# Other PSUM banks for the projections of the gated linear attention, and an earlier place in the program for five decode and mask loads

## The chip, the core and the metric

The kernel runs on one core of a Trainium2 chip. Its engines take their instructions each in a fixed order: PE (TensorE, matrix products into PSUM), DVE (VectorE), ACT (ScalarE), POOL (GpSimd) and SP (SyncE, which issues most DMAs). They wait for one another through semaphores. PSUM has 8 banks of 128 x 512 fp32, and a tile of it can be written only once the tile that lay in its bank has been read. The metric is the device time of one execution in microseconds (us).

## The reference, cut to what matters

One step of a hybrid decoder layer over a prompt of 2048 tokens and 8 samples of 8 new tokens with 4096 past tokens each. Model width 1024.

```
z = rmsnorm(h) @ w_in            # q_c, kv_c, gate_mla | q_g, k_g, v_g, a_g, gate_gla
# MLA: 8 heads, scores over 64 + 32 dims, values of 64
q_nope, q_rope = split(rmsnorm(q_c) @ w_qup);  c_kv = rmsnorm(kv_c);  k_rope = rope(kv_c)
prompt:  k = c_kv @ w_uk;  v = c_kv @ w_uv;  o = softmax(causal(q k + q_rope k_rope)) v
decode:  q_lat = q_nope @ w_uk;  c = cache_ckv[page_table], kr = cache_krope[page_table]
         o_lat = softmax(mask(q_lat c + q_rope kr)) c;  o = o_lat @ w_uv
# GLA: 4 heads, dk 64, dv 128, chunks of 64 tokens, S the carried state
o = (q exp(b)) S + A v;  S = exp(b_last) S + (k exp(b_last - b))^T v;  o = rmsnorm(o) * silu(gate)
h += concat(o_mla * silu(gate_mla), o_gla) @ w_out
h += sigmoid(h @ w_ple_gate) * (p @ w_ple_proj);  y = rmsnorm(h)
```

Outputs are y for both groups, the new latent and rotary rows, and the new GLA states.

## The kernel before, in words

The program has five stages, one after the other:

- pass_a, 0 to some 355 us: input projection for the MLA part, latents, q, k and v, which are written to DRAM (Qn, Qr, Kn, Kr, Vd).
- pass_b, to some 753 us: the GLA. For 17 tiles (16 of 128 prompt tokens, one of 64 sample tokens) inproj computes three projections of 512 columns (PSUM tiles pgB, lines 64 to 66), and gla does the chunked recurrence with PSUM tiles ptB and poB. The last step of a tile is mg (line 691, on DVE), the gated and normalised output, which SP stores to DRAM (MGd, line 692). Its factor comes from ACT (686) and POOL (91, 92). The final states go out by line 648.
- attention, first part, and decode, to some 1080 us. attention loads keys KT (lines 898 and 905), values VT (906) and queries qC (911, 912). For every head and block of 512 queries it first finds the row maxima of the scores (maxima: product on PE, line 925, into pmC; reduction on DVE, 927 to 932; the maxima are turned by PE, 940, and copied by ACT into row 96 of qC, 941), and then computes scores (955 to 957, psC), exponentials (959, 961) and outputs (968 to 970, poC). decode works on 16 chunks of 2048 past tokens: ct (latent pages, each by a DMA from SP whose address is read from the page table ptab, 764 and 769), cr and kt (indirect gathers of POOL, 771 and 775, with indices computed from pt_i and p16 at 731 to 735), products 783 and 787 into ptD. Ahead of that it needs qlat, a product of the sample queries with ukT (742), and qrs, 32 copies on DVE (750). The driver gives 3.2 attention steps for each decode step.
- attention alone, to some 1345 us.
- output, to the end: output projection, the gated embedding, the last norm.

PSUM pools take banks in the order in which they are opened, those of attention from the other end. So in pass_b pgB has banks 0 to 2, ptB 3 to 6 and poB 7; behind it ptD has 0 and 1, poD 2, poC 3, psC 4 and 5, and pmC 6 and 7.

The written order of the code is not the order on the engines. A scheduler takes all instructions of the program, with their data and buffer dependences and its own estimate of when each could run, and writes one list for every engine; a DMA into memory that no one has used can be placed anywhere ahead of its reader. On SP a DMA also waits until the one eight places ahead in its lane has landed.

Of the kernel before, what the change touches and what calls it, by code (L numbers as in the profile page):

```python
# [14 lines left out]
F32 = mybir.dt.float32  # L15
F32R = mybir.dt.float32r
I32 = mybir.dt.int32
# [4 lines left out]
PSUM = bass.MemoryType.PSUM  # L22
DRAM = bass.MemoryType.DRAM

P = 128
# [4 lines left out]
NB, TD = 8, 8  # L30
SD = NB * TD
T = S + SD
PAST = 4096
H, DN, DR, DV = 8, 64, 32, 64
CL, QL = 128, 256
# [11 lines left out]
def emit(ctx, tc, I, O):  # L47
    nc = tc.nc
# [54 lines left out]
    keep = ctx.enter_context(tc.tile_pool(name="keep", bufs=1))  # L103
# [339 lines left out]

    def pass_b(ws, xp, wb):
        with ExitStack() as c:
            wp = pool(c, "cB", 1)
            sp = pool(c, "sB", 2)
            s1 = pool(c, "s1B", 1)
            pg = pool(c, "pgB", 3, PSUM)
            pt = pool(c, "ptB", 4, PSUM)  # L450
            po = pool(c, "poB", 1, PSUM)

            def xsplit(i, m):
# [242 lines left out]
            for cnt, (i, m) in enumerate(order):  # L696
                x, x1 = x1, None
                gla(cnt, i, m, *cur)
                if cnt + 1 < len(order):
                    if cnt + 2 < len(order):  # L700
                        x1 = xsplit(*order[cnt + 2])
                    cur = inproj(x, *order[cnt + 1])
                if cnt + 2 == len(order):
                    wb.close()


    def decode(c):

# [8 lines left out]
        HP = 8  # L717
        ukT = wp.tile([P, 4, CL], F32, name="ukT")
        nc.sync.dma_start(ukT, I["w_ukT"])
        uv = wp.tile([P, H, DV], F32, name="uv")  # L720
        nc.sync.dma_start(uv, I["w_uv"].rearrange("c (h d) -> c h d", h=H))
        nmask = wp.tile([SD, NB, SD], F32, name="nmask")
        nc.sync.dma_start(nmask, I["nmask"])
        ptab = wp.tile([1, NB * 32], I32, name="ptab")
        nc.sync.dma_start(ptab, I["page_row"])
        pt_i = wp.tile([P, NB * 6 * NCK], I32, name="pt_i")
        nc.sync.dma_start(pt_i, I["pages"])
        p16 = wp.tile([P, 2], I32, name="p16")
        nc.sync.dma_start(p16, I["p16"])
        idx = wp.tile([P, NB * 2 * NCK], I32, name="idx")  # L730
# [131 lines left out]
        for n, (b, ck) in enumerate(chunks):  # L862
            cur = ld.pop(0)
            if n + 2 < len(chunks):
                ld.append(load(*chunks[n + 2]))
            if ck == 0:
                st = (sp.tile([SD, N], F32, name="mxD"), sp.tile([SD, N], F32, name="dnD"), sp.tile([SD, N, CL], F32, name="oc"))
            yield from chunk(b, ck, *cur, *st)
            if ck == NCK - 1:
                yield from fresh(b, *st)  # L870
                yield from combine(b, *st)
# [9 lines left out]

    def attention(c, we, slots):

# [6 lines left out]
        po = pool(c, "poC", 1, PSUM, side="right")  # L890
        cm = wp.tile([P, P], F32, name="cm")
        nc.sync.dma_start(cm, I["cmask"])

# [136 lines left out]
    def output(c, slots, close):  # L1030
# [118 lines left out]
            for n, (i, m) in enumerate(tiles):  # L1149
# [4 lines left out]
                hN = nx  # L1154

    with ExitStack() as wb:
        ws, xp = pass_a(wb)
        pass_b(ws, xp, wb)
    with ExitStack() as e:
        c = ExitStack()  # L1160
        slots = []
        att = attention(c, e, slots)
        next(att)
        with ExitStack() as d:
            dec = decode(d)
            acc = 0.0
            for _ in dec:
                acc += DEC_RATE
                while acc >= 1:
                    next(att, None)  # L1170
                    acc -= 1
        for _ in att:
            pass
        output(e, slots, c.close)
# [102 lines left out]
```

## Time and profile before

| | us |
|---|---|
| median of 3 runs | 1880.7 (1877.29 to 1881.57) |
| profiled execution | 1881.52 |
| its span, first to last instruction | 1879.5 |
| PE busy | 1749.4 (93%) |
| DVE busy | 1080.3 (57%) |
| ACT busy | 781.7 (42%) |
| POOL busy | 532.3 (28%) |
| mean granted clock of PE | 0.955 |

The span is 2.0 us shorter than the execution's time, and every time of the trace counts from its start. In a timeline a row has its start, its duration, the engine, the line of the kernel, the operation, the tile written and the tiles read (without the number of the buffer) and, in brackets, how long the engine stood idle ahead of it and what ended that. "issue" there means that the profile shows nothing that was waited for, "remote" a signal that it could not trace.

### The profile page before, as it was taken

Reading aid. Unit: us, or ns where it says so; the run is one execution under the profiler, and the core shown is the slowest. Engines: PE = TensorE matmul, PEld = TensorE weight load, DVE = VectorE, ACT = ScalarE, POOL = GpSimd, SP = SyncE. Lnnn points to the kernel's source line nnn. Section 1 sums busy time; section 2 is a strip of 40 time slices with the busy share of each in tenths; the row PEclk is TensorE's granted clock in tenths of the full one; section 3 lists DMA queues with packets and bytes.
Section 4 is the critical chain, followed back from the end, with each engine's and each line's share of the span. In section 5 each row is a group of like instructions: output and inputs, shape, how many; then the busy total and the mean of one; then the engine's idle time right before and its main releaser. Section 6 shows DMA issues by size and latency. Waiting matters only on the chain.

```text
span 1879.5 us, 26843 instructions
## 1 busy us (share of the span) xinstructions
PE 1749.4 (93%) x8928; PEld 1365.5 (73%) x8928; DVE 1080.3 (57%) x2359; ACT 781.7 (42%) x1896; POOL 532.3 (28%) x915
## 2 busy tenths in 40 slices
PE   4999987899999998499999999999999999999996
PEld 3877776688887786266666777777777888888884
DVE  6376476466653666466666687777777333333323
ACT  4354365343431433055554666766661212121212
POOL 5253253333442334424343011111136000000000
PEclk7999989899999998699999999999998999999998
DMA  5164475511111114655666243123334223322111
GB/s 170 40 241 140 163 272 183 170 42 40 45 40 48 32 35 121 195 157 155 184 172 171 62 129 89 49 69 77 91 84 147 89 75 88 95 85 82 56 49 34
DMA packets 187748, 200.53 MB, mean 107 GB/s; under 512 B 23290, under 2 KB 130668, under 8 KB 187612
## 3 DMA queue, kind: packets, MB, share of 16 engines
q1 hardware_dynamic: 180956, 177.86, 32.3%
q0 software_dynamic: 6656, 20.98, 3.6%
q8 instruction: 71, 1.16, 0.3%
q14 instruction: 65, 0.53, 0.1%
HBM read 142.42 MB, written 56.35 MB: 106 GB/s over the span
## 4 chain that ended last, share of the span: by engine, by line
PE 70%; DMA 3%; DVE 3%; issue 2%; SPq 1%; POOL 1%; ACT 1%; POOLq 0%; ACTq 0%; DVEq 0%
PE pgE L64 7%; PE pgE L66 7%; PE pgE L65 7%; PE pgB L66 4%; PE pgB L64 4%; PE pgB L65 4%; PE psC L955 3%; PE poC L968 3%; PE pmC L925 3%; PE poC L970 3%; PE psC L957 3%; PE psC L956 3%; PE poC L969 3%; PE ptD L783 2%; PE poD L82 1%
## 5 line engine op out<-in xcount | busy, mean ns | idle before, releaser
L959 ACT ACTIVATE ph<-psC 128x512 fp32r<-128x512 f32 (+1 forms) x320 | 171.5, 536 | 206.1 <-PE psC L957 90.1
L963 DVE TENSOR_TENSOR pl<-pf,ph 128x512 fp32r<-128x512 f32 (+1 forms) x320 | 191.3, 608 | 58.5 <-ACT pf L961 49.2
L961 ACT ACTIVATE pf<-psC 128x512 f32<-128x512 f32 (+1 forms) x320 | 170.9, 534 | 0.0
L927 DVE TENSOR_REDUCE mxC<-pmC 128x1 f32<-128x512 f32 x192 | 128.9, 684 | 54.0 <-PE pmC L925 38.1
L955 PE MATMUL psC<-qC,KT 97*128 97x512 f32 (+1 forms) x320 | 124.1, 388 | 15.4 <-issue 11.8
L966 POOL TENSOR_SCALAR_AFFINE_SELECT ph<-ph 128x128 fp32r<-128x128 f32 x128 | 43.3, 339 | 322.5 <-DVE pl L963 228.0
L968 PE MATMUL poC<-ph,VT 128*128 128x512 f32 (+1 forms) x320 | 124.3, 388 | 8.8 <-POOL ph L966 6.7
L925 PE MATMUL pmC<-KT,qC 96*128 96x512 f32 (+2 forms) x320 | 119.2, 399 | 10.1 <-issue 4.6
L970 PE MATMUL poC<-pl,VT 128*128 128x512 f32 (+1 forms) x320 | 122.0, 382 | 1.3 <-DVE pl L963 1.3
L956 PE MATMUL psC<-qC,KT 96*128 96x512 f32 (+1 forms) x320 | 119.6, 374 | 0.0
L957 PE MATMUL psC<-qC,KT 96*128 96x512 f32 (+1 forms) x320 | 119.5, 373 | 0.0
L969 PE MATMUL poC<-ph,VT 128*64 128x512 f32 (+1 forms) x320 | 118.1, 369 | 0.0
L955 PEld LDWEIGHTS psC<-qC,KT 97*128 97x128 f32 x320 | 61.3, 192 | 38.4 <-issue 13.4
L1139 DVE SCALAR_TENSOR_TENSOR thE<-thE,pgE 128x512 f32<-128x512 f32 x32 | 22.0, 688 | 114.3 <-ACT thE L1138 114.3
L64 PE MATMUL pgE<-wpg,hh 128*128 128x512 f32 x224 | 87.7, 392 | 0.0
L65 PE MATMUL pgE<-wpg,hh 128*128 128x512 f32 x224 | 87.7, 392 | 0.0
L925 PEld LDWEIGHTS pmC<-KT,qC 96*128 96x128 f32 x320 | 62.6, 198 | 32.3 <-issue 11.0
L1138 ACT ACTIVATE thE<-pgE 128x512 f32<-128x512 f32 x32 | 19.1, 598 | 160.6 <-PE pgE L66 160.6
L66 PE MATMUL pgE<-wpg,hl 128*128 128x512 f32 x224 | 85.3, 392 | 0.0
L968 PEld LDWEIGHTS poC<-ph,VT 128*128 128x128 f32 x320 | 62.7, 196 | 29.0 <-POOL ph L966 13.4
L775 POOL DMA_INDIRECT kt<-in_kropeT,idk x64 | 61.5, 961 | 65.5 <-PE ptD L787 49.5
L61 DVE TENSOR_TENSOR x<-x 128x512 fp32r<-128x512 f32 (+2 forms) x74 | 64.6, 917 | 22.8 <-PE pgB L65 14.2
(456 smaller groups left out, 4674.7 us busy)
## 6 DMA issues: line engine op xcount, KB each, us to landing
x<-in_xT SPq DMA_DIRECT2D x32, 512.0 KB
ct<-in_ckvT SPq DMA_DIRECT2D x256, 64.0 KB
x<-in_w_in SPq DMA_DIRECT2D x16, 512.0 KB
Qn<-qq SPq DMA_DIRECT2D x16, 512.0 KB
Kn<-qq SPq DMA_DIRECT2D x16, 512.0 KB
Vd<-qq SPq DMA_DIRECT2D x16, 512.0 KB
KT<-Kn SPq DMA_DIRECT2D x32, 256.0 KB
VT<-Vd SPq DMA_DIRECT2D x8, 1024.0 KB
```

Of the source, the lines that this page charges most:

```text
L64: T_.matmul(out, ah, bh, start=first, stop=False)
L65: T_.matmul(out, ah, bl, start=False, stop=False)
L66: T_.matmul(out, al, bh, start=False, stop=last)
L925: T_.matmul(ps[:, :w], qs, kv[0][cb][:96, 0, :w], start=True, stop=True)
L955: T_.matmul(ps[:, c0:], kh[:, ks], qh[:, c0:], start=True, stop=False)
L956: T_.matmul(ps[:, c0:], kh[:96, ks], ql[:, c0:], start=False, stop=False)
L957: T_.matmul(ps[:, c0:], kl[:, ks], qh[:96, c0:], start=False, stop=True)
L959: A.activation(ph[:, c0:], ps[:, c0:], AF.Exp, scale=SC)
L963: V.tensor_tensor(pl[:, c0:], pf[:, c0:], ph[:, c0:].bitcast(F32), op=ALU.subtract)
L968: T_.matmul(o[:, c0:], vt[:, kb, DV:192], ph[:, c0:], start=kb == 0, stop=False)
L969: T_.matmul(o[:DV, c0:], vt[:, kb, 0:DV], ph[:, c0:], start=False, stop=False)
L970: T_.matmul(o[:, c0:], vt[:, kb, DV:192], pl[:, c0:], start=False, stop=kb == nk - 1)
```

## The change

Three things are written differently.

1. In pass_b the three PSUM pools are opened in the order ptB, poB, pgB. ptB then has banks 0 to 3, poB 4 and pgB 5 to 7.
2. A function operands makes tiles for ukT (256 KB), nmask (128 KB), pt_i (48 KB), p16 (1 KB) in a pool of its own that is opened ahead of pass_a, and cm (64 KB, the causal mask of the maxima) in the pool that lives through the whole program. Their five loads stand in fetch, which pass_b calls at its fifth tile. decode and attention take the tiles and load them no more.
3. The load of uv stands in decode behind the second chunk, and no longer at its head.

```diff
-    def pass_b(ws, xp, wb):
+    def pass_b(ws, xp, wb, fetch):
...
-            pg = pool(c, "pgB", 3, PSUM)
+
             pt = pool(c, "ptB", 4, PSUM)
             po = pool(c, "poB", 1, PSUM)
+            pg = pool(c, "pgB", 3, PSUM)
...
                 x, x1 = x1, None
+                if cnt == 4:
+                    fetch()
                 gla(cnt, i, m, *cur)
...
+    def operands(c):
+
+        wp = pool(c, "wD0", 1)
+        e = {"ukT": wp.tile([P, 4, CL], F32, name="ukT"), "nmask": wp.tile([SD, NB, SD], F32, name="nmask"),
+             "pt_i": wp.tile([P, NB * 12], I32, name="pt_i"), "p16": wp.tile([P, 2], I32, name="p16")}
+        cm = keep.tile([P, P], F32, name="cm")
+
+        def fetch():
+            nc.sync.dma_start(e["pt_i"], I["pages"])
+            nc.sync.dma_start(e["p16"], I["p16"])
+            nc.sync.dma_start(e["ukT"], I["w_ukT"])
+            nc.sync.dma_start(e["nmask"], I["nmask"])
+            nc.sync.dma_start(cm, I["cmask"])
+        return e, cm, fetch
...
-        ukT = wp.tile([P, 4, CL], F32, name="ukT")
-        nc.sync.dma_start(ukT, I["w_ukT"])
-        uv = wp.tile([P, H, DV], F32, name="uv")
-        nc.sync.dma_start(uv, I["w_uv"].rearrange("c (h d) -> c h d", h=H))
-        nmask = wp.tile([SD, NB, SD], F32, name="nmask")
-        nc.sync.dma_start(nmask, I["nmask"])
+        ukT, nmask, pt_i, p16 = (early[k] for k in ("ukT", "nmask", "pt_i", "p16"))
         ptab = wp.tile([1, NB * 32], I32, name="ptab")
         nc.sync.dma_start(ptab, I["page_row"])
-        pt_i = wp.tile([P, NB * 6 * NCK], I32, name="pt_i")
-        nc.sync.dma_start(pt_i, I["pages"])
-        p16 = wp.tile([P, 2], I32, name="p16")
-        nc.sync.dma_start(p16, I["p16"])
+        uv = wp.tile([P, H, DV], F32, name="uv")
...
             yield from chunk(b, ck, *cur, *st)
+            if (b, ck) == (1, 0):
+                nc.sync.dma_start(uv, I["w_uv"].rearrange("c (h d) -> c h d", h=H))
...
-        cm = wp.tile([P, P], F32, name="cm")
-        nc.sync.dma_start(cm, I["cmask"])
...
+    small = ExitStack()
+    early, cm, fetch = operands(small)
     with ExitStack() as wb:
         ws, xp = pass_a(wb)
-        pass_b(ws, xp, wb)
+        pass_b(ws, xp, wb, fetch)
```

What the scheduler makes of it is seen in the lists. The changed program's line numbers are one higher in the GLA and ten higher in decode and attention (925 is 935 there). SP, the program's first 25 rows, as a difference (the rows with + are new; p is p16):

```order
 L395 DMA csn<-in_cossin 128x64
 L349 DMA cossin<-in_cossinT 128x2x64
+L717 DMA pt_i<-in_pages 128x96
+L718 DMA p_91<-in_p 128x2
+L719 DMA ukT<-in_w_ukT 128x512
+L720 DMA nmask<-in_nmask 64x512
+L721 DMA cm<-in_cmask 128x128
 L180 DMA x<-in_xT 128x2x512 x3
```

The five loads are not in the GLA. They stand behind the first and ahead of the second to fourth prompt load (in_xT) of pass_a.

PE, from the last GLA tile's first products on (ptB, poB: GLA; pmC: maxima; poD: qlat). Before:

```order
L597 MATMUL ptB_6648<-F_6642 64x64 x2
L597 MATMUL ptB_6652<-F_6642 64x64 x2
L612 MATMUL ptB_6683<-FZ160_2927,F_6676 128x128 x2
L618 MATMUL ptB_6698<-QZ0_2931,kb_6628 128x256 x2
L597 MATMUL ptB_6648<-F_6657 32x32 x4
L597 MATMUL ptB_6652<-F_6657 32x32 x4
L623 MATMUL ptB_6702<-ident_71,ke_6637 128x128 x2
L631 MATMUL poB_6707<-St1_2940,qe_6634 128x256
L640 MATMUL ptB_6716<-v_6602,kn_6705 64x128 x4
L612 MATMUL ptB_6683<-FZ80_2929,F_6688 128x128 x2
L634 MATMUL poB_6707<-v_6602,AT0_2923 128x128 x2
L631 MATMUL poB_6707<-St1_2940,qe_6634 128x256
```

And now:

```order
L598 MATMUL ptB_6661<-F_6655 64x64 x2
L598 MATMUL ptB_6665<-F_6655 64x64 x2
L935 MATMUL pmC_6810<-KT00_6780,qC_6805 128x512
L935 MATMUL pmC_6813<-KT01_6781,qC_6805 128x512
L613 MATMUL ptB_6696<-FZ160_2935,F_6689 128x128 x2
L619 MATMUL ptB_6711<-QZ0_2939,kb_6641 128x256 x2
L598 MATMUL ptB_6661<-F_6670 32x32 x4
L598 MATMUL ptB_6665<-F_6670 32x32 x4
L935 MATMUL pmC_6816<-KT02_6782,qC_6805 128x512
L935 MATMUL pmC_6819<-KT03_6783,qC_6805 128x128
L624 MATMUL ptB_6715<-ident_71,ke_6650 128x128 x2
L641 MATMUL ptB_6729<-v_6615,kn_6718 64x128 x4
```

Before, all of the last GLA tile stands ahead of the first maxima. Now nine of the first block's sixteen products stand between its rows (two here behind its second row), and the rest behind it, around the two groups of L742.

PE, from the last of these maxima to the first scores. Before (ptD: decode's products; psC: scores):

```order
L925 MATMUL pmC_6846<-KT02_6771,qC_6794 128x512
L783 MATMUL ptD_7198<-ct_7018,qlat_6919 64x512 x4
L925 MATMUL pmC_6849<-KT03_6772,qC_6794 128x512
L787 MATMUL ptD_7198<-kt_7019,qrs_6932 128x512 x2
L940 MATMUL pmC_6858<-identr_73,m4r_6856 1x128 x4
L925 MATMUL pmC_6982<-KT00_6769,qC_6869 128x512
L955 MATMUL psC_6873<-qC_6794,KT00_6769 128x512
```

And now:

```order
L935 MATMUL pmC_6857<-KT02_6782,qC_6805 128x512
L935 MATMUL pmC_6860<-KT03_6783,qC_6805 128x512
L950 MATMUL pmC_6869<-identr_73,m4r_6867 1x128 x4
L935 MATMUL pmC_6984<-KT00_6780,qC_6880 128x512
L965 MATMUL psC_6884<-qC_6805,KT00_6780 128x512
```

decode's first products, L783 and L787, stood ahead of L940 and are now behind three groups of scores and two of outputs. Two more rows have changed their place at this point. On SP the store of the last tile's MGd now stands behind the loads of ptab and uv and directly ahead of the page-table read for ct; before, the loads of uv, nmask, ptab, pt_i and p16 stood between. On POOL the gathers of cr and kt follow the last tile's line 92 as before. The five loads behind GLA's end are gone there.

More of the change, by code (lines that the diff above doesn't have):

```diff
@@ L704, in pass_b, with decode @@
                     wb.close()
-    def decode(c):
+    def operands(c):
[10 more added lines that the diff above has]
+        return e, cm, fetch
+    def decode(c, early):
         wp = pool(c, "wD", 1)
@@ L879, in decode, with attention @@
         yield
-    def attention(c, we, slots):
+    def attention(c, we, slots, cm):
         wp = pool(we, "wC", 1, side="right")
@@ L1161, in emit @@
         slots = []
-        att = attention(c, e, slots)
+        att = attention(c, e, slots, cm)
         next(att)
         with ExitStack() as d:
-            dec = decode(d)
+            dec = decode(d, early)
             acc = 0.0
@@ L1171, in emit @@
                     acc -= 1
+        small.close()
         for _ in att:
```

## The prediction

> **What bounds the kernel now.** I read the windows first. Between 750 and 800 us, where the gated linear attention (GLA) ends and the prompt attention begins, PE is busy 22.34 us of 50; in the 300 us behind it, 292.72. PE takes its instructions in a fixed order there, so a microsecond won before 800 has 300 us of nearly full PE work to keep it. Columns: window, length, busy us of PE, PEld, DVE, ACT, POOL, then granted clock, DMA share, GB/s.
>
> ```profile
> 750.00:800.00 50.00, 22.34 (x64) 12.25 (x65) 21.16 (x71) 2.82 (x11) 22.26 (x24) 0.64 0.68 192
> 755.00:760.00 5.00, 0.77 (x1) 0.29 (x1) 3.52 (x10) 0.00 (x0) 1.17 (x2) 0.68 1.00 254
> 775.00:780.00 5.00, 0.99 (x4) 0.34 (x3) 1.59 (x3) 0.00 (x0) 3.78 (x5) 0.50 0.96 285
> 790.00:795.00 5.00, 0.00 (x0) 0.00 (x0) 0.00 (x0) 0.00 (x0) 3.78 (x5) 0.59 0.31 87
> 800.00:1100.00 300.00, 292.72 (x1759) 203.51 (x1759) 192.86 (x596) 165.06 (x355) 95.94 (x162) 0.96 0.55 152
> ```
>
> Then PE's timeline over the same stretch (start, duration, line, what it waited for in brackets):
>
> ```profile
> 742.10 0.54 PE L597 MATMUL ptB<-F 64*64 64x64 f32 x8 [2.48 <-DVE F L585]
> 752.60 0.61 PE L634 MATMUL poB<-v,AT 128*128 128x128 f32 x4
> 752.96 0.48 PE L925 MATMUL pmC<-KT,qC 96*128 96x512 f32 x1
> 757.52 0.77 PE L925 MATMUL pmC<-KT,qC 96*128 96x512 f32 x1 [4.08 <-issue]
> 762.84 1.97 PE L742 MATMUL poD<-qTs_n,ukT 64*128 64x64 f32 x8 [4.55 <-DMA ukT<-in_w_ukT]
> 767.46 1.22 PE L925 MATMUL pmC<-KT,qC 96*128 96x512 f32 x2
> 769.04 1.18 PE L925 MATMUL pmC<-KT,qC 96*128 96x512 f32 x2 [0.36 <-DVE mxC L927]
> 779.98 3.68 PE L783 MATMUL ptD<-ct,qlat 128*64 128x512 f32 x8 [3.83 <-DMA ct<-in_ckvT]
> 784.24 1.13 PE L787 MATMUL ptD<-kt,qrs 64*128 64x512 f32 x4
> 785.58 0.40 PE L940 MATMUL pmC<-identr,m4r 128*1 128x128 f32 x4 [0.21 <-issue]
> 798.08 0.80 PE L955 MATMUL psC<-qC,KT 97*128 97x512 f32 x1 [11.82 <-issue]
> 814.20 1.94 PE L783 MATMUL ptD<-ct,qlat 128*64 128x512 f32 x8
> 816.07 1.13 PE L787 MATMUL ptD<-kt,qrs 64*128 64x512 f32 x4
> ```
>
> Four holes: 4.08 us at the second maximum (L925), 4.55 at L742 for ukT, 3.83 at L783 for the first latent pages ct, 11.82 before the first scores (L955). The other engines say what ends the first and the last.
>
> ```profile
> 756.29 1.13 DVE L691 SCALAR_TENSOR_TENSOR mg<-poB,ssB,gtB 128x128 f32<-128x128 f32 x4 [4.74 <-POOL ssB L92]
> 759.55 5.74 DVE L750 COPY qrs<-qTs_r 32x64 f32<-32x64 f32 x29
> 768.29 1.29 DVE L927 TENSOR_REDUCE mxC<-pmC 128x1 f32<-128x512 f32 x2
> 788.32 1.22 DVE L793 TENSOR_REDUCE m<-ptD 128x1 f32<-128x1024 f32 x1 [2.77 <-remote]
> 769.03 1.24 POOL L771 DMA_INDIRECT cr<-in_ckv,idx  x1 [12.77 <-DVE mxC L927]
> 795.55 0.94 POOL L775 DMA_INDIRECT kt<-in_kropeT,idk  x1 [0.30 <-issue]
> 797.45 0.58 ACT L941 ACTIVATE qC<-pmC 1x512 fp32r<-1x512 f32 x1 [29.50 <-remote]
> ```
>
> The mg of the last GLA tile ends at 757.42, and 0.1 us later the second maximum starts: its PSUM bank was the old poB or ptB. The 11.82 us are stranger. L940 was done at 785.98, but ACT picked its result up (L941) only at 797.45, although ACT had nothing else. From 769.03 to 796.49 POOL issued 22 indirect gathers (L771, L775) in a row, 1.25 us apart; signals between engines arrive promptly until some 776 and then late (L793 waits 2.77 us for a PE result) until the burst is over. I call this the **gather tax**. Why it exists no row says; that it ends with the burst does.
>
> **The change, part by part.** Last, SP:
>
> ```profile
> 720.80 0.33 SPq L892 DMA_DIRECT2D cm<-in_cmask  x1
> 740.34 0.60 SPq L912 DMA_DIRECT2D qC<-Qr  x1
> 759.64 0.54 SPq L719 DMA_DIRECT2D ukT<-in_w_ukT  x1
> 761.17 0.51 SPq L723 DMA_DIRECT2D nmask<-in_nmask  x1
> 762.23 0.35 SPq L727 DMA_DIRECT2D pt_i<-in_pages  x1
> 762.62 0.42 SPq L729 DMA_DIRECT2D p<-in_p  x1
> 765.73 36.51 SPq L769 DMA_DIRECT2D ct<-in_ckvT  x32
> ```
>
> *Banks.* With pgB on the last three banks, the maxima's banks come free when the last projection has been evacuated, before 742. The scheduler therefore puts the first two maxima among the last GLA tile's matmuls, right behind L597 (742.10 + 0.54 = 742.6). They now wait for their data instead: KT and qC come in the same order on SP as before, the last of them issued at 740.34, and in the trace the packets of that load end at 745.6. PE is in order, so L612, L618 and the rest queue behind that wait: **+3.0 us** on the tail. The tail took 753.21 − 742.64 = 10.6 us. Nine maxima now stand in it; each costs about 0.6 us of PE (1.22 for two) and 0.65 us of DVE (1.29 for two), 5.4 us of PE, of which the tail's own PE idle takes perhaps 1.5. The tail ends near 745.6 + 10.6 + 3.9 = 760. Behind that PE owes the two L742 (3.9 us) and seven maxima, DVE more: about eight reductions (5.2 us), L750 and its memset (7.3 us, which ran under the ukT wait before), mg 1.1, indices and small ones 2: 15.6 us. So the maxima end near 776, and with L940 and ACT's copy the scores could start at **778** against 798.08.
>
> *Order.* Before, L783 and L787 stand ahead of L940; now they stand behind three groups of scores and two of values. They are still owed: 3.68 + 1.13 us at the half clock of that place, 1.94 + 1.13 later at the full one; I take 4. Net, at best: 798.1 − 778 − 4 = **−16 us**.
>
> *Gather tax.* The page numbers pt_i are there early, so the gathers no longer wait for them, only for the last tile's POOL row (L92), ahead of them in order; by the tail above that is near 764, and a burst of 18 then ends near 764 + 18 × 1.25 = 787. The 769-to-776 stretch of before, where maxima still ran promptly (0.36 us waits), was the first 7 us of the burst; 7 us after 764 is 771, with five maxima, L940 and ACT's copy still to come. Bounds: no tax at all (0), or hand-off only after the burst, psC at 789.5 (11.5, about the 11.4 that L941 lost). I take three late hand-offs at the 2.77 us of L793: **+8**, nearer the upper end since the mechanism moves with the burst.
>
> *Five loads to the front.* The tiles never wait for memory, so the scheduler does not leave fetch in the GLA: the five loads stand in SP's first twenty rows, ahead of the second to fourth prompt load.
>
> ```profile
> 12.00:16.00 4.00, 3.99 (x11) 2.30 (x9) 3.10 (x5) 3.67 (x8) 0.32 (x2) 1.00 1.07 370
> 14.15 0.63 ACT L185 ACTIVATE acc<-x 128x512 f32<-128x512 f32 x1 [0.33 <-DMA x<-in_xT]
> 33.30 0.47 PE L291 MATMUL pt<-ident,nat 64*128 64x64 f32 x2 [17.31 <-DVE nat L274]
> ```
>
> Issue: 0.35 + 0.42 + 0.54 + 0.51 + 0.33 = 2.15 us of SP. Bytes: 497 KB at 370 GB/s, 1.4 us, at a place where the DMA engines are full and ACT just waits for x. Against it, PE stands still from 16.0 to 33.30 behind a chain over POOL and DVE, and in the new order one of POOL's 1.25 us adds (L189) comes behind that chain's links. Bounds −1.25 and +2.15; I take **+0.7**. The cover they lose nothing of: removed at the transition, they give SP 1.8 us back (0.54 + 0.51 + 0.35 + 0.42), which is inside the next term. cm's place at 720.80 cost nothing, for the KT load behind it waits for the projection anyway.
>
> *ct behind MGd.* On SP the store MGd of the last tile (waiting for mg) now stands directly ahead of the page-table read and all ct loads; before, mg was done by then. mg near 766, so ct starts near 767 instead of 765.73: 1.3 us, hidden, because L783 now comes some 10 us of attention behind the first scores. uv is read at decode's end only: nothing.
>
> In the old order no gather was ahead of ct; now three are, from 764 on. The page's DMA queues (packets, MB, share) give their size:
>
> ```profile
> q0 software_dynamic: 6656, 20.98, 3.6%
> ...
> L775 POOL DMA_INDIRECT kt<-in_kropeT,idk x64 | 61.5, 961 | 65.5 <-PE ptD L787 49.5
> ```
>
> The Trainium skill ("DMA: Bandwidth & Descriptors", Issuing engines are not separate DMA queues) says that DMAs issued by different engines run on the same 16 DMA engines and interleave; it speaks against an earlier burst. By it, all seven or eight gathers that run before and beside the first chunk's loads, 0.22 MB each (20.98 MB over 64 kt and 32 cr), would at the 285 GB/s of 775 to 780 us bring ct up to 6 us later than its 780.4, to 786; that is inside the cover (788), and the sum would stay.
>
> **Sum:** −16 + 8 + 0.7 = −7.3. The profiled execution took 1881.5 us (span 1879.5 and 2.0 around it), 0.8 over the median 1880.7 of the runs, so about **1874** profiled, 1873.4 on the median's scale; I say 1874. A difference under 0.2% (3.8 us) can't be told from none here: faster means below 1877, slower above 1884.5.
>
> **The rivals.**
>
> *A, no gather tax on the maxima.* The late signals start 7 us into the burst or depend on ct traffic too; if maxima and L941 stay prompt, the whole −16 + 0.7 holds: 1866. For it: waits of 0.3 us up to 776. Against: those were the burst's first 7 us.
>
> *B, ct late.* The chain of waits has the end of the first chunk's loads and, above it, what a qC load took:
>
> ```profile
> 751.95 7.07 DMA qC<-Qn
> ...
> 773.04 6.08 DMA ct<-in_ckvT
> ```
>
> The first 16 ct loads went out in 9.4 us before (765.73 to 775.1, by their single records), the second 16, inside the taxed stretch, took the rest of the 36.51 us: 27 us, 1.7 each. Were the first chunk's all at that pace from 767, the last would be issued at 794 and land, with the 6.08 us of the chain, at 800. L783 then blocks PE, in order, when the attention ahead of it (from 786 on, 10 us) is done at 796; L787's end is near 804, against some 806 for the same work before. With the start-up's upper end, 2.15, the gain is gone: 1881. For it: the burst starts before ct now. Against: were the pace set by the eight loads in flight and not by the burst, it would have been as slow for the first sixteen.
>
> *C, the maxima hold the GLA.* Mechanism: PE waits in order at the first L925 for qC, and all of the last tile, so mg, MGd, L92 and the gathers, ct and L783, hang behind it. It decides once the data come 2 us later than 745.6; by the 7.07 us above they could be there at 748. Then the tail ends at 762.5, mg at 768.5, ct starts at 769.5, goes out by 797 at 1.7 us a load and lands at 803; L787 ends at 807 and chunk 0's transposes (1.1 us) come only then: 2 us worse than the 806 of before, with 2.15 at the start +4, 1886. For it: DVE's reductions stand ahead of the last tile's own copies too. Against: KT and qC loads have kept their order.
>
> *D, the change doesn't do what it says.* Partly so: the loads lie at the start, not in the GLA. What is left of the price is the start-up term, and the wait for ukT is gone either way.
>
> **Chances.** Forecast 0.43 (1870 to 1877), A 0.23, B 0.21, C 0.13. Four fifths lie between 1862 (A with the start-up's gain and some microseconds of clock) and 1884. Faster by over 0.2%: forecast, A: 0.66; the same: most of B, 0.19; slower: C and a little of B, 0.15.
>
> **What would show it.** PE: first L925 near 745 with a DMA wait of about 3 us; last L634 near 760; no wait for ukT; L955 between 778 and 790, ahead of L783. POOL: gathers from 764. ACT: the remote wait of L941, short (A) or until the burst's end. SP: ct from 767, 9 us or 27 for sixteen. Start: L291 within 2 us of 33.3. It is wrong if L955 isn't before 790, if L783 waits more than 5 us for ct, or if the time behind 810 differs by more than the shift there.

## The result, and the profile after

The changed kernel took 1892.33 us (median of 19 runs, 1883.32 to 1900.38), the kernel before beside it 1880.7 (19 runs, 1874.19 to 1885.65): a ratio of 1.0062, 95% interval 1.0048 to 1.0075. It is slower by 11.6 us, on the other side of the forecast 1874 and outside its range of 1862 to 1884. The profiled execution's span is 1888.6 us against 1879.5.

To see where, I use one measure besides the views. Every matrix product in the trace has its number of streamed columns; summed over time, this tells how much work PE has done. The **offset** at a time of the kernel before is how much later the other kernel's PE reaches the same work.

| offset (us) at | 35 | 200 | 300 | 378 | 711 | 880 | 930 | 1040 | 1700 |
|---|---|---|---|---|---|---|---|---|---|
| after, against before | +2.1 | +4.8 | +4.8 | +10.1 | +9.7 | +0.2 | +5.4 | +7.9 | +9.4 |

So: 4.8 us are lost in the first pass, 5.3 at the start of the second, 9.5 won at the transition, and 7.7 of these given back between 880 and 1040. The windows of the changed kernel show two of the places (columns as in the prediction):

```profile
320.00:340.00 20.00, 11.30 (x30) 7.04 (x30) 13.22 (x21) 9.88 (x14) 6.08 (x12) 0.67 0.88 315
750.00:800.00 50.00, 28.37 (x111) 19.52 (x111) 29.13 (x94) 7.80 (x27) 21.79 (x24) 0.61 0.78 209
800.00:1100.00 300.00, 286.01 (x1711) 195.93 (x1712) 185.46 (x572) 159.10 (x341) 99.37 (x158) 0.95 0.55 154
880.00:1040.00 160.00, 149.28 (x901) 101.28 (x900) 96.48 (x298) 79.13 (x173) 63.71 (x99) 0.94 0.63 172
```

and the same windows of the kernel before, where the prediction did not show them:

```profile
320.00:340.00 20.00, 20.00 (x82) 16.26 (x81) 9.94 (x15) 6.24 (x11) 6.18 (x12) 0.92 0.84 301
880.00:1040.00 160.00, 154.21 (x924) 105.30 (x923) 101.76 (x314) 82.51 (x178) 60.97 (x97) 0.96 0.61 166
```

Between 750 and 800 PE does 6 us more work than before, as meant. Behind 800 it does 6.7 us less in 300, and between 320 and 340 it is busy for 11.30 us of 20. PE's timeline of the changed kernel at these places:

```profile
35.46 0.73 PE L291 MATMUL pt<-ident,nat 64*128 64x64 f32 x4 [20.12 <-DVE nat L274]
...
343.46 0.47 PE L64 MATMUL pgB<-w,x 128*128 128x512 f32 x1 [1.02 <-DVE qq L61]
...
751.17 0.80 PE L598 MATMUL ptB<-F 64*64 64x64 f32 x8 [2.42 <-DVE F L586]
757.01 1.19 PE L935 MATMUL pmC<-KT,qC 96*128 96x512 f32 x2 [5.05 <-DMA qC<-Qr]
...
770.36 1.97 PE L752 MATMUL poD<-qTs_n,ukT 64*128 64x64 f32 x8
...
787.75 0.59 PE L950 MATMUL pmC<-identr,m4r 128*1 128x128 f32 x4 [3.88 <-DVE mxC L942]
...
789.01 0.79 PE L965 MATMUL psC<-qC,KT 97*128 97x512 f32 x1
...
803.27 3.68 PE L793 MATMUL ptD<-ct,qlat 128*64 128x512 f32 x8 [7.42 <-DMA ct<-in_ckvT]
...
923.55 0.69 PE L935 MATMUL pmC<-KT,qC 96*128 96x384 f32 x1 [3.51 <-DVE mxC L937]
```

The first product of the second pass is the row at 343.46. In the kernel before it was this one, 21 us earlier, among the first pass's last products:

```profile
322.05 0.63 PE L64 MATMUL pgB<-w,x 128*128 128x512 f32 x1
```

SP, ACT, POOL and DVE of the changed kernel:

```profile
734.50 7.14 SPq L908 DMA_DIRECT2D KT<-Kr  x8
...
750.85 0.60 SPq L922 DMA_DIRECT2D qC<-Qr  x1
...
778.60 18.59 SPq L779 DMA_DIRECT2D ct<-in_ckvT  x14
...
788.37 0.58 ACT L951 ACTIVATE qC<-pmC 1x512 fp32r<-1x512 f32 x1 [12.58 <-issue]
790.69 0.60 ACT L969 ACTIVATE ph<-psC 128x512 fp32r<-128x512 f32 x1 [1.74 <-DMA ct<-in_ckvT]
...
801.54 0.60 ACT L969 ACTIVATE ph<-psC 128x512 fp32r<-128x512 f32 x1 [8.14 <-remote]
...
775.84 1.24 POOL L781 DMA_INDIRECT cr<-in_ckv,idx  x1 [2.36 <-DVE idk L745]
...
797.37 0.94 POOL L785 DMA_INDIRECT kt<-in_kropeT,idk  x1 [0.30 <-issue]
...
921.85 0.94 DVE L991 RECIPROCAL rcC<-rcC 16x128 f32<-16x128 f32 x1 [8.19 <-issue]
```

The wait for ukT is gone, and the first scores start at 789.01 against 798.08, 9 us earlier although the stage began 9.7 us late. But PE then stands for ct (7.42). ACT takes up the third group of scores, which PE had finished at 794.71, only at 801.54, 3.2 us behind the end of the burst's last gather (798.31). Its earlier hand-offs in the same burst were prompt: L951 starts at 788.37, 0.03 us after PE's L950 ended (788.34) and 12.5 us after the first gather. So in this order the first block's maxima and their copy paid no gather tax.

The prediction read the same burst of the kernel before as late from some 776 on. Rows of PE and DVE there show a product (783.59 + 0.72 = 784.31) that DVE took up 0.03 us later, 15.3 us after the first gather at 769.03:

```profile
783.59 0.72 PE L925 MATMUL pmC<-KT,qC 96*128 96x512 f32 x1
...
784.34 0.56 DVE L930 TENSOR_REDUCE mxC<-pmC 128x1 f32<-128x384 f32 x1 [7.47 <-issue]
```

At 921.85 DVE has stood 8.19 us for rcC, the sums of the softmax: their load stands on SP behind seven loads of ct. In the kernel before, DVE's row of the same line has a shorter wait:

```profile
923.70 0.94 DVE L981 RECIPROCAL rcC<-rcC 16x128 f32<-16x128 f32 x1 [3.65 <-DMA rcC<-Dd]
```

### The profile page after: what moved, and what is told of

It is laid out like the page before. It is cut to its first block, busy times and chain, and to the rows that moved or that the text cites. A ratio compares the mean times of both kernels' runs of the same rounds, so it can differ in the third digit from the quotient of the medians.

```text
span 1888.6 us, 26822 instructions
## 1 busy us (share of the span) xinstructions
PE 1747.5 (93%) x8928; PEld 1360.3 (72%) x8928; DVE 1084.4 (57%) x2359; ACT 783.1 (41%) x1896; POOL 536.3 (28%) x915
## 4 chain that ended last, share of the span: by engine, by line
PE 67%; DVE 4%; DMA 4%; issue 3%; SPq 2%; ACT 1%; POOL 1%; POOLq 0%; DVEq 0%; ACTq 0%
PE pgE L64 7%; PE pgE L66 7%; PE pgE L65 7%; PE pgB L64 4%; PE pgB L65 4%; PE pgB L66 4%; PE poC L978 3%; PE psC L965 3%; PE pmC L935 3%; PE poC L980 3%; PE psC L967 3%; PE psC L966 3%; PE poC L979 3%; PE ptD L793 1%; PE poD L82 1%
## 5 line engine op out<-in xcount | busy, mean ns | idle before, releaser
L935 PEld LDWEIGHTS pmC<-KT,qC 96*128 96x128 f32 x320 | 61.7, 196 | 34.3 <-DVE mxC L937 11.4
L978 PEld LDWEIGHTS poC<-ph,VT 128*128 128x128 f32 x320 | 62.4, 195 | 28.3 <-POOL ph L976 14.5
```

The source lines that it names most:

```text
L935: T_.matmul(ps[:, :w], qs, kv[0][cb][:96, 0, :w], start=True, stop=True)
L978: T_.matmul(o[:, c0:], vt[:, kb, DV:192], ph[:, c0:], start=kb == 0, stop=False)
```

## The experiments

They ran in four groups, each on one chip, with the kernel before beside it: 1880.1, 1854.5, 1879.1 and 1878.4 us. Ratios are to the kernel before on the same chip; offsets are against its profile of the first measurement, except where another kernel is named.

### Group 1: the parts alone (the kernel before: 1880.1 us)

**banks_only**: the kernel before with only the new order of the three pools.

```diff
-            pg = pool(c, "pgB", 3, PSUM)
             pt = pool(c, "ptB", 4, PSUM)
             po = pool(c, "poB", 1, PSUM)
+            pg = pool(c, "pgB", 3, PSUM)
```

> The kernel before with nothing but the order of the three GLA pools changed (ptB, poB, pgB); all loads where they were. Theory 1 (my reading of the trace after: the loss has two places ahead of the transition, 5 us inside pass_a from the list that the early loads shuffled, and 5.4 us at the start of pass_b, where the projection banks 5 to 7 are still held by pass_a's query and key products): pass_a as before, the first pgB product some 15 to 21 us later than its 322 us, the GLA 5 to 6 us later from then on; time 1881 to 1887. Theory 2 (the whole loss comes from the early loads, the banks alone gain): first pgB product near 322 us and 1865 to 1877.

Measured: 1881.56 us (10 runs), ratio 1.0015 (1.0001 to 1.0029). Offsets: −1.9 at 300, +0.6 at 378, −11.9 at 880, −0.2 at 1040, +0.8 at the end. The banks alone win 14 us between 711 and 880 and lose nearly all of it by 1040. The time lies in theory 1's range, and pgB's first product comes late as theory 1 has it, in a kernel whose first pass is as before:

```profile
339.17 0.77 PE L64 MATMUL pgB<-w,x 128*128 128x512 f32 x1 [2.92 <-DVE qq L61]
```

But this costs 2.5 us between 300 and 378, not 5 to 6.

**loads_only**: the changed kernel with the old order of the pools.

> The changed kernel with the old bank order (pgB, ptB, poB); the five loads early. Theory 1: pass_a ends some 5 us late as in the changed kernel, the first pgB product comes early again, ahead of pass_a's last products; the wait for ukT (4.55 us) is gone at the transition; 1877 to 1886. Theory 2 (early loads are the whole loss): 1888 to 1893.

Measured: 1890.69 us (4 runs), ratio 1.0067 (1.0045 to 1.0088). Offsets: +3.1 at 35, +6.5 at 300, +4.0 at 378, +2.5 at 880, +12.0 at 1040, +9.5 at the end. Of the two parts this is the dear one, and 6.5 us of it are lost before 300. The first pass's list has changed beyond the five loads: near 185 us PE waits three times for splits of DVE that stood earlier before. The time is in theory 2's range, but its other half, that the banks alone gain, did not come. pgB's first product is early again (328.98), and between 300 and 378 this kernel wins 2.5 us where the changed one loses 5.3.

**sides_t7**: the pools of pass_b in the old order; instead attention's PSUM pools lie on the low banks and decode's and the output's on the high ones; and the tiles of the five loads are opened between the two passes, cm among them, so that the loads can only go out in the GLA.

```diff
-        cm = keep.tile([P, P], F32, name="cm")
+        cm = wp.tile([P, P], F32, name="cm")
...
-        pt = pool(c, "ptD", 1, PSUM)
-        po = pool(c, "poD", 1, PSUM)
+        pt = pool(c, "ptD", 1, PSUM, side="right")
+        po = pool(c, "poD", 1, PSUM, side="right")
...
-        pm = pool(c, "pmC", 2, PSUM, side="right")
+        pm = pool(c, "pmC", 2, PSUM)
...
-    early, cm, fetch = operands(small)
     with ExitStack() as wb:
         ws, xp = pass_a(wb)
+        early, cm, fetch = operands(small)
         pass_b(ws, xp, wb, fetch)
```

> The same intention by other means: pass_b keeps its bank order; attention's PSUM pools are opened from the low banks and decode's from the high ones, so that the maxima's banks are those of pgB; the operand pool is opened between pass_a and pass_b, in memory that pass_a used, so that the five loads can't move ahead of the GLA. Theory 1: no loss up to 750 us (last pgB product within 1 us of 724.5), so what is left is the transition alone: 1870 to 1881. Theory 3 (the transition loses by itself, since the first maxima stop PE in the middle of the last GLA tile until qC has landed and ct comes late behind mg): 1882 to 1890.

Measured: 1882.16 us (8 runs), ratio 1.0 (0.997 to 1.0029). The runs lie in two bunches, three from 1869.08 to 1873.01 and five from 1881.88 to 1886.72; the profile, at 1884.47, is of the upper one, and what sets the bunches apart is not known. Offsets: +0.1 at 300, −0.7 at 378, −16.0 at 880, −1.1 at 1040, +3.1 at the end (there PE waits 3.8 us for a list of the output stage that came out differently). Both early losses are gone, the transition wins 17 us, and 15 of them are given back in the same 160 us. So in this execution the give-back isn't a matter of either early loss.

**after_nogather**: the changed kernel without its 96 indirect gathers; kt and cr are tiles of zeros, so decode leaves out the cached rotary scores and the cached values.

```diff
+        zk = wp.tile([P, 512], F32, name="kt")
+        zc = wp.tile([P, 2, 8, CL], F32, name="cr")
...
-                G.indirect_dma_start(cr[:, e].rearrange("p a c -> p (a c)"), None, I["ckv"],
```

> The changed kernel without the 96 indirect gathers: cr and kt are one pair of zeroed tiles, so the cached rope scores and the values of decode are left out of the result. Theory 1 (the late signals and the slow ct loads at the transition are caused by the burst of gathers): sixteen ct loads go out in 8 to 11 us instead of some 21, L793 waits less than 1 us for ct, ACT takes up results at once, and the time is 8 to 15 us below the changed kernel's. Rival (the eight loads in flight set the pace of ct, and the late signals come from the ct traffic itself): ct at the same 1.3 us each, time within 4 us of the changed kernel's.

Measured: 1862.83 us (4 runs), ratio 0.9929 (0.9905 to 0.9954). Offsets: +8.9 at 711, −14.5 at 880, −18.7 at 1040, −16.5 at the end. Against a kernel before that still has its gathers, the transition wins 23 us and nothing is given back. The time is 29.5 us under the changed kernel's first 1892.33, twice the upper end of the theory; its sign on ct came (34 to 38 loads in the 20 to 22 us up to 800 here and in the repeat of group 4). Group 4 compares both kernels without gathers.

### Group 2, where the kernel before took 1854.5 us

**t7**: the change, with the tiles of the five loads opened between the passes (the last lines of the diff of sides_t7), the bank order as changed.

> The change, but with the tiles of the five early loads opened between the two passes, so that the loads can only go out in the gated linear attention; the bank order of the second pass is the changed one. Theory (the change loses in three places: up to 6 us in the first pass by the early loads, about 5 us where the second pass's projections must wait for the first pass's last banks, and the transition's gain is given back between 880 and 1040 us): the first pass is as before (offset 0 at 300 us), 2 to 5 us are lost between 322 and 378, the whole is 1883 to 1887. Rival (the early loads cost nothing and the first pass's 5 us are the noise of one profile): still 1890 to 1893, with the offset of 5 us at 300. Second rival (with the first pass mended, the gain of the transition stays): 1874 to 1878.

Measured: 1863.98 us (4 runs), ratio 1.006 (1.0037 to 1.0084): 9.5 us slower than the kernel before here. Read as distances from 1880.7, that is outside the theory's 2 to 6 and just inside its rival's 9 to 12; but the rival's sign, an offset of 5 at 300, didn't come. Against before_rc (below) on the same chip its offsets are +1.7 at 300, +4.4 at 378, −2.1 at 880, +5.7 at 1040, +5.5 at the end; its profiled execution (1856.89) is 7.1 under its median.

**sides_t7_rc** and **before_rc**: sides_t7 and the kernel before, each with one more edit. The reciprocals of the softmax sums are taken once for each block of 512 queries, for all heads, when the last head is done. The seven loads of sums in mid-attention, and DVE's waits for them, are gone; the two DRAM tiles are laid out by block for it.

```diff
-            if h == H - 1 or j == 0:
-                n = 4 if h == H - 1 else 16
-                view = slice(j * 512, j * 512 + n * P)
-                rc = sp.tile([16, P], F32, name="rcC")
-                nc.sync.dma_start(rc[:n], Dd[h, view].rearrange("(a b) -> a b", b=P))
-                V.reciprocal(rc[:n], rc[:n])
+            if h == H - 1:
+                rc = sp.tile([32, P], F32, name="rcC")
+                nc.sync.dma_start(rc, Dd[j].rearrange("h (a b) -> (h a) b", b=P))
+                V.reciprocal(rc, rc)
```

> The variant with the maxima's banks free and the loads in the GLA (1882.2 us), and the reciprocals of the softmax sums taken once per block of 512 queries at the end of the attention, for all heads together, instead of once per head: seven loads of the sums, which stood on SP among the ct loads, and the DVE waits for them are gone. Theory (the gain of 16 us at 880 is given back mainly because VectorE stands in order behind that load, 7.6 us, and PE, ACT behind VectorE): the offset at 1040 stays at -7 or lower and the whole is 1872 to 1877. Rival (the decode's supply, gathers and page loads, sets the pace of 880 to 1040; a removed wait only shows the next one): offset back at -3 to 0 at 1040, whole 1880 to 1883.

> The kernel before with the same edit of the reciprocals, as a control of that edit alone. There the wait of VectorE for the sums was 3.65 us and PE lost little by it. Theory of the wait: 1878 to 1880, a smaller gain than in the variant with free banks. Rival (the supply of the decode sets the pace): 1879 to 1882, the same as before within the noise.

Measured: sides_t7_rc 1852.15 us (10 runs), ratio 0.9983 (0.9968 to 0.9997); before_rc 1851.38 (10 runs), 0.9989 (0.9978 to 1.0). The absolute times expected came from another chip and don't apply. Between the two the offset is +1.7 at 711, −3.2 at 880, −2.1 at 1040, +0.1 at the end: on this chip there are only 5 us to win at the transition, and 1.1 of them are given back by 1040. t7, which keeps the loads of the sums (and has other banks), gave back 7.8 there.

**before_nogather**: the kernel before without the gathers (the same parts of decode left out).

> The kernel before without the 96 indirect gathers (the cached rope keys and cached values of the decode are zeros, so its output leaves them out). The changed kernel lost 29 us without them. Theory (the gathers tax the transition and the stretch to 1100 alike in both kernels, and without them the transition's gain of the change would show): before without gathers 1860 to 1868, that is above the changed kernel's 1862.8 minus its losses of 10 us before 711. If the gathers cost before only some 10 us (rival: the change itself made the gathers dear, by starting them earlier), it is 1868 to 1874.

Measured: 1854.05 us (10 runs), ratio 1.0008 (0.999 to 1.0026). On this chip the gathers cost **nothing**, which neither theory had. The reason is in before_rc's trace. Up to 806 us its lists are those of the kernel before, and POOL issues the same burst of gathers, 1.25 us apart; but PE and ACT hand over promptly in the middle of it, where the kernel before waited. PE, ACT and POOL of before_rc:

```profile
784.12 0.40 PE L940 MATMUL pmC<-identr,m4r 128*1 128x128 f32 x4 [0.27 <-DVE mxC L919]
...
785.19 0.50 PE L955 MATMUL psC<-qC,KT 97*128 97x512 f32 x1 [0.39 <-ACT qC L941]
...
784.56 0.58 ACT L941 ACTIVATE qC<-pmC 1x512 fp32r<-1x512 f32 x1 [17.34 <-PE pmC L940]
...
783.13 0.94 POOL L771 DMA_INDIRECT cr<-in_ckv,idx  x1 [0.30 <-issue]
```

The first scores wait 0.39 us here, 11.82 in the profile that the prediction read.

### Group 3: the same chip for before and after (1879.1 us)

**before_2** and **after_2**: the two kernels once more.

> The kernel before once more, for a profile on the chip that runs the kernels of this group. The last group ran on another chip than the first: the kernel before took 1854.5 us there, 26 us less, and the hole of 11.8 us before the first scores was not there in a kernel with the same instructions up to that place, though POOL issued the same burst of gathers. Theory (the late hand-off during the gathers belongs to the chip): either the hole is there and the time is near 1880, or it is not and the time is near 1855; nothing between. Rival (it belongs to how the execution falls, on any chip): hole and time don't go together.

> The changed kernel once more, on the same chip as the next two. Theory (the losses, start-up and first pass 6 us, the second pass's first projections 2 to 5 us, stretch from 880 to 1040 us 8 us, don't depend on the chip, the gain at the transition does): on a chip without the hole the change is slower by 12 to 17 us (ratio 1.007 to 1.009); on a chip with it, by 11 us as first measured. Rival (the change's order is as good where hand-offs are prompt): within 4 us of before.

Measured: before_2 1872.91 (one run, at the lower end of the 19 beside it, 1872.73 to 1884.41; the hole is there, 9.1 us of PE before the first scores), after_2 1892.28 (4 runs), ratio 1.0068 (1.0044 to 1.0092). after_2 against before_2: +6.0 at 300, +12.1 at 378, +11.5 at 711, −1.0 at 880, +4.5 at 930, +13.1 at 1040, +13.7 at the end. The same four places as in the first measurement, with a larger give-back.

**after_rc** and **t7_rc**: the changed kernel, and t7, with the edit of the reciprocals.

> The changed kernel with the reciprocals taken once for all heads at the end of the attention: no load of the sums stands among the ct loads on SP, and VectorE doesn't wait for it in order (8.2 us at L991 in the changed kernel). Theory (that wait is most of what the change loses between 880 and 1040): 6 to 9 us below the changed kernel on the same chip. Rival (the stretch is paced by the decode's supply): 0 to 3 us below, as much as the same edit gave the kernel before (3 us).

> The same edit, with the tiles of the five early loads opened between the passes, so that the loads go out in the gated linear attention and the first pass is as before. Theory (the early loads at the kernel's start cost the first pass 5 us): 4 to 6 us below the changed kernel with the reciprocal edit on the same chip, and what is left against the kernel before with that edit is the 3 us at the second pass's start. Rival (the 5 us of the first pass were noise): within 2 us of it.

Measured: after_rc 1882.75 us (10 runs), ratio 1.0019 (1.0003 to 1.0035), 9.5 below after_2; the theory's 6 to 9 and a little more. Its profiled execution is only 1.7 us shorter than that of after_2 (that one was 6.3 under its median, this one 1.4 above); the offset between them shows the place: +1.2 at 900, −7.7 at 930, then back to −1.9 at 1040. Both theories are partly right: the wait is worth 8.9 us where it stands, and something behind it takes most of that in this execution. t7_rc: 1877.81 (10 runs), 0.9986 (0.9969 to 1.0002), 4.9 below after_rc, as expected: the loads at the start cost the first pass 5 us (in the two profiles t7_rc is 5.8 ahead at 300). With both removed the change is no longer slower than the kernel before, which by the edit of the reciprocals alone gains 4.0 in group 4.

### Group 4: what the gathers take (1878.4 us)

> The kernel before without its 96 gathers (rope scores and values of the cached tokens are left out). Theory (chips differ in the late hand-offs beside gathers and in nothing else that counts here): on a chip where the kernel before takes 1880 us, this takes 1853 to 1860, 20 to 27 less, and the hole before the first scores is under 2 us; on a chip where it takes 1855, within 3 us of it as before. Rival (the chips differ elsewhere, in memory or clock): on a chip of 1880 us it falls by less than 12 us.

> The changed kernel without its gathers, on the same chip. Theory: what is left is the change's own losses, 5 us in the first pass and 2 to 5 at the second pass's start, less the 4 to 5 us wait for ukT: slower than the kernel before without gathers by 3 to 9 us, 1858 to 1866. Rival (the change's order is a gain once the gathers are out of the way): below the kernel before without gathers.

> The variant with the maxima's banks free, the loads in the GLA and the reciprocals once at the end. On the chip of 1854.5 us it took 1852.2. Theory (the wait for the sums and the gathers' late hand-offs both eat the transition's gain): on a chip of 1880 us 1871 to 1876, some 4 to 9 us below the kernel before, 2 to 6 us below the changed kernel with its loads in the GLA and the same edit (1877.8). Rival (the gathers of the chunks from 930 on take the whole gain whatever is freed): 1876 to 1880.

> The kernel before with the reciprocals once at the end, on the same chip as the variant above. Theory: the wait was 3.65 us there (4.3 in the repeat), so 2 to 4 us below the kernel before. Rival (on a chip with late hand-offs the wait stands beside a gather series, and the edit frees as much as in the changed kernel, 9.5 us): 7 to 10 us below.

| | us (runs) | ratio, interval |
|---|---|---|
| before_nogather_2 | 1859.08 (5) | 0.9899 (0.9869 to 0.9928) |
| after_nogather_2 | 1864.89 (7) | 0.9931 (0.991 to 0.9952) |
| sides_t7_rc_2 | 1872.86 (10) | 0.9962 (0.9944 to 0.9979) |
| before_rc_2 | 1874.41 (10) | 0.997 (0.9954 to 0.9986) |

All four times came out as the theory had them. Without gathers the kernel before falls by 19.3 us here, to within 5 of what it takes on the chip of group 2; the changed one stays 5.8 us slower. The edit of the reciprocals gives the kernel before 4.0 us. sides_t7_rc is the fastest full version here, 5.5 us under the kernel before, but the edit alone gives 4 of these.

The traces of the two kernels without gathers qualify this. The offset of after_nogather_2 to before_nogather_2 is +14.5 at 711, +9.4 at 880, +15.6 at 1040 and +16.0 at the end (the latter's profile, at 1848.9, is 10.2 under its median, so the whole is too large against the 5.8 of the medians). Of the 5 us that the changed order wins at the transition it gives back 6 by 1040 with no gather at all, and PE waits once for 3.34 us there, for DVE's L938 (at 1008.20). So the gathers are not the only thing behind 880 that takes the gain.

The same programs have now been profiled on two chips, so the offsets between two executions of one program tell what a chip of the slower kind takes, and where:

| group 4 against group 2 | 378 | 711 | 880 | 930 | 1040 | 1700 |
|---|---|---|---|---|---|---|
| before_rc | −0.9 | −0.9 | +15.9 | +19.2 | +23.4 | +22.9 |
| sides_t7_rc | −1.8 | −0.5 | +3.5 | +7.5 | +21.0 | +21.8 |
| before_nogather | +0.6 | −1.3 | −0.2 | +0.3 | +0.2 | −1.9 |

In the old order 16.8 us of the tax fall into the transition and 7.5 behind 880. With free banks 4.0 fall into the transition and 17.5 behind it. The sum is 24.3 and 21.5. **For sides_t7_rc the gain at the transition was in the main the tax moved, not removed**. The changed kernel itself was not run on the chip of group 2, so for it this is carried over and not measured. It also has the loads of the sums in its way: after_rc is 9.5 us faster without them. How its 7.7 us divide between the two was not separated. How it is paid at the new place, by sides_t7_rc on the two chips; first group 2 (the window, then PE, ACT and POOL):

```profile
930.00:1040.00 110.00, 108.70 (x694) 74.95 (x693) 71.34 (x232) 59.74 (x130) 34.08 (x58) 1.00 0.56 154
...
944.67 1.80 PE L82 MATMUL poD<-cr,pT 128*64 128x128 f32 x29
...
946.52 0.27 ACT L824 ACTIVATE oc<-poD 64x128 f32<-64x128 f32 x1 [3.65 <-PE poD L82]
...
948.61 0.94 POOL L785 DMA_INDIRECT kt<-in_kropeT,idk  x1 [0.30 <-issue]
```

and group 4:

```profile
930.00:1040.00 110.00, 105.63 (x597) 72.44 (x597) 62.72 (x192) 51.88 (x109) 32.16 (x50) 0.88 0.49 132
...
952.53 1.80 PE L82 MATMUL poD<-cr,pT 128*64 128x128 f32 x29
959.10 0.33 PE L833 MATMUL poD<-cTs,qlat 128*64 128x64 f32 x2 [1.75 <-issue]
...
958.45 0.27 ACT L824 ACTIVATE oc<-poD 64x128 f32<-64x128 f32 x1 [7.72 <-PE pmC L935]
...
956.47 0.94 POOL L785 DMA_INDIRECT kt<-in_kropeT,idk  x1 [0.30 <-issue]
```

In group 2 PE ends at 946.47 and ACT takes the result at 946.52, with three gathers still to come. In group 4 PE ends at 954.33, and ACT starts at 958.45, 1.0 us after the last of four gathers has ended (957.41); PE waits for it in order at L833. A wait like it stands at 997.35, shorter ones between. PE is idle only 3.1 us longer in this window (4.37 against 1.30), so the greater part of the 13.5 us between 930 and 1040 goes with the lower granted clock, 0.88 against 1.00.

## Why the prediction was wrong

- *"A microsecond won before 800 has 300 us of nearly full PE work to keep it"*: this premise failed, and with the two early losses below it turned the sign. Against the forecast −7.3 the offset at the end is +9.4: 7.7 are the give-back, 5.3 the start of the second pass, 4.1 the loads at the start beyond +0.7, and 1.5 came behind 1040, less 1.5 that the transition won beyond −8 and 0.4 between 378 and 711. The transition term itself, −16 + 8 = −8, came close to the 9.5 us measured between 711 and 880; that is luck in its second part, as the next point says. It was taken for a gain of the whole, and 7.7 us (14.1 in the repeat) went again by 1040. PE was busy for 292.72 of those 300 us, so a gain would have been kept if PE's list alone set the pace. What I didn't look at is what PE's partners wait for there: gathers at every chunk, and a load of sums behind ct on SP that DVE waits for in order. Busy time of before doesn't show the waits that a new order brings.
- *Gather tax*: rightly seen as the price of the burst (without gathers the kernel before is 19.3 us shorter in group 4). But the +8 was put on three late hand-offs of the maxima, because only the first 7 us of the burst were read as prompt. The first block's maxima paid nothing: L951 was taken up within 0.03 us, as rival A had it, and the scores started at 789.01, which less the stage's 9.7 is 779, near the "at best" of 778. Of the −16, 6.5 us were then lost behind the first scores, where ct and the exponentials came late and the sum had no term. It was wrong in two more ways. It was there in three of the four groups and not in group 2, with the same instructions; one profile could not tell that. And it is paid by whatever hand-off meets a series of gathers: I priced only the maxima's, and the later chunks' series took much of what the first burst left.
- *Five loads to the front*, +0.7 with an upper bound of 2.15: the start lost 2.1, three times the term and at its bound (L291 at 35.46, 2.16 late, forecast within 2). It missed another 2.7 us, which arise between 160 and 200, where the scheduler's lists had changed. I followed the five loads and POOL's L189 in the first rows, but not the lists behind. The 5 us in all agree with t7_rc against after_rc (4.9).
- *Banks*: a whole term is missing. Banks 5 to 7, where pgB now lies, are those of pass_a's pqA, the last tiles that pass_a reads (pqA stands third in its pool order, lines 154 to 156). So pgB's first product waits until 343.46, and the interleaving of the two passes is lost: +5.3 us (banks_only: +2.5, t7: +2.7; sides_t7, with the old order there: −0.8). The banks alone account for some 2.5; the rest appears only together with the late first pass, and why was not tried. I had looked at which banks the pool frees at its end, and not at which it takes over at its start.
- *Rivals B and C* both happened, each about as described. C: KT's loads go out from 734.50 and not from 724.74, so qC's data decide the first maxima (5.05 us, forecast 3.0), in the middle of the last tile. The prediction let that decide from 2 us on; it was 11.4 (757.01 less 745.6), of which 9 to 10 are the lateness of the stage. B: 14 ct loads took 18.59 us and L793 waited 7.42. That wait is over the 5 us that the prediction named as a sign of being wrong. Neither made the loss: the transition as a whole still won 9.5 us by 880.
- *ct sharing the DMA engines with the gathers*: by the Trainium skill ("DMA: Bandwidth & Descriptors", Issuing engines are not separate DMA queues) ct was estimated to land at 786; PE got it at 803.27, with the first load 11 us later than forecast (778.2 against 767). The other 6 us are not bandwidth alone: between 795 and 800 the DMA share of the changed kernel is 0.50 and between 800 and 805 it is 0.17, while PE still waits. And in group 2 before_rc issued 55 ct loads in the 35.17 us from 764.93 on, beside its burst, and the same program in group 4 only 33 in 37.12.
- *D* was right: the loads lie at the start. I had put nothing on what that costs beyond the start-up.

The chances: faster at 0.66 and slower at 0.15 rested on rivals that all sit in the transition. No case gave a place outside it a loss above 2.15 us.

## What to carry to other kernels

When pools change banks, look at both ends: who held the new banks ahead of the pool, and who gets the old ones. A gain at one place is kept only if nothing downstream is paced by something that hasn't moved; ask of the next hundreds of microseconds which loads and hand-offs the other engines wait for, not how busy PE was. And where a wait has no visible cause ("issue", "remote"), find out whether it is the program's or the chip's before pricing a change by it.

## What the runs showed of the hardware

- Chips differed here in how late a hand-off between engines comes while POOL issues a series of indirect gathers. In three groups a result of PE could wait until the series had ended (11.5 us at the first burst in the first profile, 4.1 at a series of four), in one it didn't. Not every hand-off in a series is late: at the first burst they were prompt for some 15 us (to 784.34 in the kernel before, to 790.69 in the changed one) and late behind that, and at the series of four from its second gather on. In the traces this is 24.3 us of the kernel with the old order. Without gathers the offsets of the same program on the two kinds agree within 2 us, in one execution each; the medians are 5.0 apart. Each chip was used in one sitting, so the chip and its state at that time are not told apart. Why it happens, no trace says.
- In group 4 the issue of DMAs on SP was slower too during a burst: 1.12 us for each ct load (37.12 us, 33 loads) against 0.64 (35.17, 55) in group 2. Whether it is the same late signal was not tried.
- Executions of one program spread by up to 17.6 us here (sides_t7, 1869.08 to 1886.72), so single profiles place a loss better than they size it.
